# A hybrid attention layer on one core: an unused table of taps is dropped, x arrives in five first pieces, and every engine gets a new order of issue

## The chip, the cores and the metric

One core of a Trainium2 chip. The time is the device time of one execution in microseconds (us), the median of several runs. Before the change it is 332.9 us (3 runs, 332.89 to 332.98).

## The reference

One layer over 256 tokens of width 1024, in float32. The input is projected by one wide matrix, and the columns go to four mixers; their outputs are joined, projected, normed, and followed by a feed-forward stage of width 4096.

```python
h = x @ w_in
(q_n, kc, vc, ks, vs, kw, vw, g_n, q_m, k_m, v_m, conv_in, q_h, f_h, i_h, g_h) = split(h)
kc = nsa_compress(kc, cmp_pe[0], cmp_w1[0], cmp_b1[0], cmp_w2[0])    # and vc with [1]
o_nsa  = nsa_attention(q_n, kc, vc, ks, vs, kw, vw, sigmoid(g_n), rel_tab)
o_moba = moba_attention(q_m, k_m, v_m, rel_tab)
o_conv = conformer_conv(conv_in, dw_w, dw_b, cln_g, cln_b, pw_w)     # 31 taps, causal
o_hgrn = hgrn2_mixer(q_h, f_h, i_h, g_h, lb, hn_g)
mixed = concatenate([o_nsa, o_moba, o_conv, o_hgrn], -1) @ w_out
x = layer_norm(ALPHA * x + mixed, ln1_g, ln1_b)
ff = square(relu(x @ w_ff1)) @ w_ff2
return layer_norm(ALPHA * x + ff, ln2_g, ln2_b)
```

## The kernel before

**Stages.** The input projection is cut into chunks of columns (`ca`, `cg` for the convolution, `n1` and `ni` for the keys, values and gates, `qn`, `f`, `q`, `g`, `km`, `qm`, `vm`). Their products are mixed with the four mixers' own work up to about 130 us; then come `w_out`, the first norm, and 16 groups of the feed-forward stage, each a product with 256 columns of `w_ff1` and one with 256 rows of `w_ff2`.

**Precision.** Most weights and activations are split: ScalarE writes a rounded high part (`..._hi`, L245), VectorE the remainder (`..._lo`, L246), and TensorE takes three products per tile (L313 to L315 for transposed results, L335 to L337 for the chunk `ni`). The chunks `ca`, `cg`, `qn` and `km` are multiplied unsplit (L520, L310), as two passes each.

**Memory and queues.** A weight goes from HBM into one of five 1 MB buffers (the pool `raws`), requested from SyncE's queue (L228, and L424 for the two 1 MB pieces of each `nsa_cmp_w1`, `w1` for short). A buffer is free again when the last reader of its tenant is done: VectorE's remainder for a split weight, TensorE's last product for an unsplit one. x itself (`xf`) is requested from ScalarE's queue in four pieces (`FIRST`, L272), the first weight `w_ca` in the same four. GpSimd's queue loads the small constants, and among them `tapw`, a table of convolution taps of 1 MB which no instruction reads, since the convolution is done on VectorE (L573, 60 instructions of one tap each).

**Warm-up.** Seven products of a zeroed tile (L292) run on TensorE before the first piece of x is there.

**The first norm.** For each token tile t (two of them): two halves of x + mixed (L1014), their statistics (L1016, L1019), the inverse root of the variance (L1022 to L1026), a diagonal matrix `scale` of it (L1044), and two halves of (x - mean) * gain (L1042). TensorE then writes the norm's bias into PSUM by a small product (L1048, four in all, `pts[t][c]`), and adds x transposed and scaled on top (L1051, 16 products, each recorded as two rows). ScalarE (L1058) and VectorE (L1059) split the result for the feed-forward stage, which starts with L1089.

**Order.** Nothing is left to a scheduler: the table `ISSUE` lists for every engine the numbers of its instructions in the order in which they are issued, and `issue_in` ties each to the one before it. An engine works strictly in that order.

Of the kernel before, what the change touches and what calls it, by code (L numbers as in the profile page):

```python
# [17 lines left out]
P = 128  # L18
S = 256
# [27 lines left out]
def shape_constants():  # L47
# [13 lines left out]
    for i, b in enumerate(LEVELS):  # L61
# [48 lines left out]
    ),  # L110
    DVE=(
# [13 lines left out]
    ),  # L125
    Activation=(
# [9 lines left out]
    ),  # L136
# [1080 lines left out]
```

## Time and profile before

| | |
|---|---|
| median of 3 runs | 332.9 us |
| the profiled execution, its own time | 335.78 us |
| its span, first to last instruction | 334.0 us |
| TensorE (PE) busy | 319.8 us |
| VectorE (DVE) busy | 233.3 us |
| ScalarE (ACT) busy | 166.8 us |
| bytes moved by DMA | 62.75 MB |

The profiled execution took 2.9 us more than the median of the other runs. Starts of instructions are given in us from the span's start; an instruction's end on TensorE is modelled, and its rows overlap, so the start of the next row tells how fast they follow one another. "Idle before" in brackets is the time for which the engine had nothing under way, and behind the arrow stands what ended it.

### The profile page before, as it was taken

What the parts mean: (1) busy time and instruction counts of PE and PEld (TensorE: products, weight loads), DVE (VectorE), ACT (ScalarE), POOL (GpSimd) and SP (SyncE); (2) the same over time, 40 slices, a digit from 0 to 9 for tenths busy, and PEclk for the clock granted to TensorE, in tenths of its full rate; (3) what the DMA queues carried; (4) which work ended last, traced back from release to release, by engine and by line L of the source; (5) the groups of instructions that cost most, each with busy time, mean ns of one, the idle gap of its engine ahead of it and who ended that gap; (6) DMA issues with size and microseconds to landing.
All of it is one profiled execution on the core that took longest, in us unless ns stands there. A gap on an engine that the chain in (4) does not pass through costs nothing.

```text
span 334.0 us, 4992 instructions
## 1 busy us (share of the span) xinstructions
PE 319.8 (96%) x1929; PEld 273.1 (82%) x1929; DVE 233.3 (70%) x428; ACT 166.8 (50%) x307; POOL 10.5 (3%) x33
## 2 busy tenths in 40 slices
PE   8999969999999999989999999999999999999990
PEld 6897859898988778788888888888888888888880
DVE  0269969999989866886677477747564756568286
ACT  1464444784899982344365354535453545373100
POOL 3500000000000100000000000100000000000000
PEclk9999998999999999999999999999999999999996
DMA  7999799094300216556567555965565646520012
GB/s 234 387 398 416 235 395 388 15 371 135 121 0 2 54 74 251 153 226 186 214 232 251 176 203 155 318 202 207 153 226 160 219 144 233 156 98 0 2 49 77
DMA packets 18359, 62.75 MB, mean 188 GB/s; under 512 B 1784, under 2 KB 3664, under 8 KB 17696
## 3 DMA queue, kind: packets, MB, share of 16 engines
q1 hardware_dynamic: 15648, 56.61, 47.8%
q0 software_dynamic: 1056, 3.72, 3.2%
q10 hardware_dynamic: 1632, 2.11, 2.2%
q8 instruction: 15, 0.25, 0.3%
q14 instruction: 8, 0.07, 0.1%
HBM read 61.37 MB, written 1.06 MB: 187 GB/s over the span
## 4 chain that ended last, share of the span: by engine, by line
PE 86%; DVE 8%; DMA 2%; ACT 1%; issue 1%; DVEq 0%; ACTq 0%
PE mm L1102 15%; PE mm L1100 8%; PE hg L1121 5%; PE hg L1122 4%; PE tt L1122 4%; PE tt L1120 4%; PE hg L1120 4%; PE tt L1121 4%; DMA w_q_raw<-in_w_in_dram 2%; PE mm_km L310 2%; PE mm L1099 2%; PE mm_cg L310 2%; DVE yc L573 2%; PE acc L292 1%; PE tt L371 1%; PE tt L397 1%
## 5 line engine op out<-in xcount | busy, mean ns | idle before, releaser
L1102 PE MATMUL mm<-x1s,w_hi 128*128 128x512 f32 x210 | 74.4, 394 | 0.0
L246 DVE TENSOR_TENSOR r_lo<-r_raw,r_hi 128x1024 fp32r<-128x1024 f32 x40 | 47.4, 1221 | 24.8 <-ACT r_hi L245 24.8
L1100 PE MATMUL mm<-x1s,w_lo 128*128 128x256 f32 x240 | 61.0, 279 | 0.0
L245 ACT ACTIVATE r_hi<-r_raw 128x1024 fp32r<-128x1024 f32 x40 | 40.6, 1050 | 33.5 <-PE tt L1122 32.4
L1100 PEld LDWEIGHTS mm<-x1s,w_lo 128*128 128x128 f32 x240 | 44.9, 188 | 2.7
L1102 PEld LDWEIGHTS mm<-x1s,w_hi 128*128 128x128 f32 x210 | 39.2, 188 | 7.4
L246 DVE TENSOR_TENSOR w_lo<-w_raw,w_hi 128x1024 fp32r<-128x1024 f32 x32 | 37.8, 1218 | 5.0 <-ACT w_hi L245 5.0
L245 ACT ACTIVATE w_hi<-w_raw 128x1024 fp32r<-128x1024 f32 x32 | 32.2, 1051 | 4.6 <-DMA w_raw<-in_w_ff_dram 4.5
L1106 ACT ACTIVATE fx<-mm 128x256 f32<-128x256 f32 x30 | 11.4, 383 | 44.4 <-PE mm L1102 44.4
L1107 DVE TENSOR_TENSOR fs<-mm,fx 128x256 f32<-128x256 f32 x30 | 12.6, 424 | 28.5 <-ACT fx L1106 28.5
L573 DVE SCALAR_TENSOR_TENSOR yc<-hc,cols,yc 128x256 f32<-128x256 f32 x60 | 27.5, 479 | 0.5
L1121 PE MATMUL hg<-r_lo,fh 128*128 128x512 f32 (+1 forms) x70 | 26.4, 378 | 0.0
L1120 PE MATMUL hg<-r_hi,fh 128*128 128x512 f32 (+1 forms) x70 | 26.4, 377 | 0.0
L1121 PE MATMUL tt<-r_lo,fh 128*128 128x512 f32 x64 | 24.1, 396 | 0.0
L1122 PE MATMUL hg<-r_hi,fl 128*128 128x512 f32 (+1 forms) x70 | 22.4, 376 | 0.0
L1122 PE MATMUL tt<-r_hi,fl 128*128 128x512 f32 x64 | 20.8, 397 | 0.0
L1120 PE MATMUL tt<-r_hi,fh 128*128 128x512 f32 x64 | 20.8, 396 | 0.0
L1121 PEld LDWEIGHTS hg<-r_lo,fh 128*128 128x128 f32 x70 | 13.2, 189 | 2.7
L1122 PEld LDWEIGHTS hg<-r_hi,fl 128*128 128x128 f32 x70 | 13.2, 189 | 2.6
L1120 PEld LDWEIGHTS hg<-r_hi,fh 128*128 128x128 f32 x70 | 13.2, 188 | 2.1
L1121 PEld LDWEIGHTS tt<-r_lo,fh 128*128 128x128 f32 x64 | 12.1, 188 | 2.9
L1122 PEld LDWEIGHTS tt<-r_hi,fl 128*128 128x128 f32 x64 | 12.1, 189 | 2.8
(331 smaller groups left out, 650.7 us busy)
## 6 DMA issues: line engine op xcount, KB each, us to landing
w_raw<-in_w_ff_dram SPq DMA_DIRECT2D x32, 512.0 KB, 4.4
r_raw<-in_w_ff_dram SPq DMA_DIRECT2D x16, 1024.0 KB, 4.9
w<-in_nsa_cmp_w_dram SPq DMA_DIRECT2D x4, 1024.0 KB, 7.6
r_raw<-in_w_out_dram SPq DMA_DIRECT2D x4, 1024.0 KB, 6.1
w_ni_raw<-in_w_in_dram SPq DMA_DIRECT2D x2, 792.0 KB, 11.4
xf<-in_xt_dram ACTq DMA_DIRECT2D x4, 256.0 KB, 6.9
w_ca_raw<-in_w_in_dram SPq DMA_DIRECT2D x4, 256.0 KB, 7.1
w_cg_raw<-in_w_in_dram SPq DMA_DIRECT2D x2, 512.0 KB, 5.8
```

The lines of the kernel that those rows point to most:

```text
L245: A.activation(self.h[:, i:j], self.raw[:, i:j], AF.Copy)
L246: self.last = V.tensor_tensor(self.l[:, i:j], self.raw[:, i:j], self.h[:, i:j].bitcast(F32), op=ALU.subtract)
L310: T.matmul(dst[:, i], w.raw[:, k, P * i:P * i + P], xf[:, k], start=(k == 0), stop=(k == KT - 1))
L573: V.scalar_tensor_tensor(yc[:, i], h, w, yc[:, i], op0=ALU.mult, op1=ALU.add)
L1099: T.matmul(flat(pf[i]), h, flat(x1s[:, k]), start=True, stop=False)
L1100: T.matmul(pf[i][:, 0], l, x1h[:, k], start=False, stop=False)
L1102: T.matmul(flat(pf[i]), h, flat(x1s[:, k]), start=False, stop=(k == KT - 1))
L1106: A.activation(lo[:, i], pf[i][:, 1], AF.Copy)
L1107: V.tensor_tensor(sq[:, i], pf[i][:, 0], lo[:, i], op=ALU.add)
L1120: T.matmul(bank_, h, w.h[:, i, sl], start=(g == 0 and i == 0), stop=False)
L1121: T.matmul(bank_, h, w.l[:, i, sl], start=False, stop=False)
L1122: last = T.matmul(bank_, l, w.h[:, i, sl], start=False, stop=(g == NG - 1 and i == 1 and sl.stop != 768))
```

## The change

1. The table `taps`, its load and the branches that would read it are gone.
2. The first of the two 1 MB pieces of `w1` for c = 0 goes into the space that the table had (tag `mixl`), not into a buffer of `raws`, and it is requested much earlier, right behind `w_qn`.
3. x and `w_ca` come in five first pieces: two of one k-tile, three of two k-tiles.
4. There are five warm-up products where there were seven.
5. The last bias product of the first norm, (t, c) = (1, 1), is issued six times into the same PSUM bank. The first five start and end a group of their own, so that the sixth overwrites them.
6. `ISSUE` has a new table for all five engines.

```diff
-    FIRST, X_LATE = ((0, 2), (2, 4), (4, 6), (6, 8)), 2
+    FIRST, X_LATE = ((0, 1), (1, 2), (2, 4), (4, 6), (6, 8)), 2
...
-    for _ in range(7):
+    for _ in range(5):
         T.matmul(pidle, idle[:, :P], idle, start=True, stop=True)
...
-            raw = raws.tile([P, 2048], F32, name="w1", tag="raw").rearrange("p (a b) -> p a b", a=8)
+
+            pool, tag = (raws, "raw") if c or i else (wk, "mixl")
+            raw = pool.tile([P, 2048], F32, name="w1", tag=tag).rearrange("p (a b) -> p a b", a=8)
             nc.sync.dma_start(raw, I["nsa_cmp_w1"][:, c, i])
...
-    tapw = wk.tile([P, 8, 8, 32], F32, name="tapw", tag="mixl")
-    late(tapw, I["taps"])
...
         for c in range(2):
-            T.matmul(pts[t][c], bsum, bhot[:, 4 * c:4 * c + 4, None].to_broadcast([40, 4, P]), start=True, stop=False)
+            to = pts[t][c], bsum, bhot[:, 4 * c:4 * c + 4, None].to_broadcast([40, 4, P])
+
+            for _ in range(5 if (t, c) == (1, 1) else 0):
+                T.matmul(*to, start=True, stop=True)
+            T.matmul(*to, start=True, stop=False)
...
     SP=(
-        "0-10 30 28-29 11-27 31-89 "
+        "0-11 17 31 29-30 12-16 18-28 32-90 "
```

**SyncE's queue, the loads up to `w_km`.** Before (names `w_150` and `w_152` are the two pieces of `w1` for c = 0, `DMAHW` a wait for an earlier transfer, `PE` and `DVE` a wait for a buffer that these engines still read):

```order
L228 DMA w_qn_raw<-in_w_in_dram 128x1024 [waits DMAHW6_49]
L930 DMA pw<-in_conv_pw_w_dram 128x2x256 [waits DMAHW7_49]
L690 DMA w_687<-in_nsa_cmp_w_dram 128x128 [waits DMAHW0_49]
L692 DMA w2k<-in_nsa_cmp_w_dram 128x256 [waits DMAHW1_49]
L228 DMA w_f_raw<-in_w_in_dram 128x1024 [waits DMAHW2_49,PE_49]
L228 DMA w_f_raw<-in_w_in_dram 128x1024 [waits DMAHW3_49]
L228 DMA w_ni_raw<-in_w_in_dram 128x1584 [waits DMAHW4_49,PE_49]
L228 DMA w_qm_raw<-in_w_in_dram 128x1024 [waits DMAHW5_49,DVE_49]
L228 DMA w_qm_raw<-in_w_in_dram 128x1024 [waits DMAHW6_49]
L424 DMA w_150<-in_nsa_cmp_w_dram 128x2048 [waits DMAHW7_49,DVE_49]
L424 DMA w_152<-in_nsa_cmp_w_dram 128x2048 [waits DMAHW0_49,PE_49]
L228 DMA w_q_raw<-in_w_in_dram 128x1024 [waits DMAHW4_49,DMAHW2_49,DVE_49]
```

and now:

```order
L424 DMA w_150<-in_nsa_cmp_w_dram 128x2048 [waits DMAHW1_49]
L905 DMA pw<-in_conv_pw_w_dram 128x2x256 [waits DMAHW2_49]
L665 DMA w_685<-in_nsa_cmp_w_dram 128x128 [waits DMAHW3_49]
L667 DMA w2k<-in_nsa_cmp_w_dram 128x256 [waits DMAHW4_49]
L226 DMA w_f_raw<-in_w_in_dram 128x1024 [waits DMAHW5_49,PE_49]
L226 DMA w_f_raw<-in_w_in_dram 128x1024 [waits DMAHW6_49]
L226 DMA w_ni_raw<-in_w_in_dram 128x1584 [waits DMAHW7_49,DVE_49]
L226 DMA w_qm_raw<-in_w_in_dram 128x1024 [waits DMAHW0_49,PE_49]
L226 DMA w_qm_raw<-in_w_in_dram 128x1024 [waits DMAHW1_49]
L424 DMA w_152<-in_nsa_cmp_w_dram 128x2048 [waits DMAHW2_49,DVE_49]
L226 DMA w_q_raw<-in_w_in_dram 128x1024 [waits DMAHW4_49,PE_49]
L226 DMA w_q_raw<-in_w_in_dram 128x1024 [waits DMAHW6_49]
```

`w_150` needs no buffer of the pool any more, so each later load finds another buffer: `w_q` had waited for VectorE, which makes the remainder of the second half of `w_ni`, and now waits for TensorE's last product with `w_qn`.

**VectorE at the first norm, from the last halves of x + mixed (`mm` for t = 0, `tt` for t = 1) to the last (x - mean) * gain.** Before (`nw` the inverse root, `scale_1471` the diagonal of t = 0, `scale_1498` that of t = 1):

```order
L1019 BN_AGGR mv<-st 128x2
L1042 SCALAR_TENSOR_TENSOR x_1341<-x_1341,mv,gb 128x512 x2
L1014 SCALAR_TENSOR_TENSOR x_1341<-x_1341,tt 128x512
L1022 TENSOR_SCALAR nw<-mv 128x1
L1025 SCALAR_TENSOR_TENSOR nw<-nw 128x1
L1016 BN_STATS st<-x_1341 128x6
L1026 TENSOR_SCALAR nw<-nw 128x1
L1044 TENSOR_SCALAR scale_1471<-cc,nw 128x128
L1014 SCALAR_TENSOR_TENSOR x_1341<-x_1341,tt 128x512
```

and now (`scale_1469` is that of t = 0, `scale_1496` that of t = 1):

```order
L989 SCALAR_TENSOR_TENSOR x_1339<-x_1339,tt 128x512
L991 BN_STATS st<-x_1339 128x6
L994 BN_AGGR mv<-st 128x2
L1017 SCALAR_TENSOR_TENSOR x_1339<-x_1339,mv,gb 128x512
L997 TENSOR_SCALAR nw<-mv 128x1
L1000 SCALAR_TENSOR_TENSOR nw<-nw 128x1
L1001 TENSOR_SCALAR nw<-nw 128x1
L1019 TENSOR_SCALAR scale_1496<-cc,nw 128x128
L1001 TENSOR_SCALAR nw<-nw 128x1
L1019 TENSOR_SCALAR scale_1469<-cc,nw 128x128
L1017 SCALAR_TENSOR_TENSOR x_1339<-x_1339,mv,gb 128x512 x3
```

All of tile 0's work was done ahead of the last half of tile 1. Now both of its (x - mean) * gain and its `scale` stand behind `scale` of tile 1: the three at the end are t = 0, t = 1, t = 0. On TensorE the 16 products went tile 0 (`acc`, `hg`), then tile 1 (`hg`, `acc`); now they go tile 1 (`hg`), tile 0 (`hg`), tile 1 (`acc`), tile 0 (`acc`), behind the nine bias products.

On ScalarE around 30 us, before: both halves of `w_f_hi`, the copy of `qn` out of PSUM, then the high part of the second half of `w_ni`. Now that high part stands ahead of the copy of `qn`.

## Rows read from the trace of the kernel before

**Rows 1.** The page: busy time, share of the span and instructions of each engine.

```profile
PE 319.8 (96%) x1929; PEld 273.1 (82%) x1929; DVE 233.3 (70%) x428; ACT 166.8 (50%) x307; POOL 10.5 (3%) x33
```

**Rows 2.** Waits of TensorE, 0 to 150 us: line, waited for, total, times, longest.

```profile
PE mm_q L313 <- ACT iv L345: 2.6, 1, 2.6
PE hg L1051 <- DVE scale L1044: 1.3, 1, 1.3
```

**Rows 3.** Chain of waits, 25 to 60 us: start, us, what.

```profile
37.27 1.81 DVE w_ni_lo L246
39.10 7.20 DMA w_q_raw<-in_w_in_dram
46.40 1.06 ACT w_q_hi L245
```

**Rows 4.** Waits of SyncE's queue, 0 to 60 us.

```profile
SPq L228 <- DVE w_ni_lo L246: 5.8, 1, 5.8
```

**Rows 5.** Stretches: busy time by engine, granted clock, DMA share, GB/s.

```profile
28.00:34.00 6.00, 5.31 (x27) 4.46 (x26) 5.86 (x14) 4.47 (x8) 0.00 (x0) 1.00 1.03 398
...
46.00:48.00 2.00, 0.00 (x0) 0.00 (x0) 0.51 (x1) 1.56 (x5) 0.00 (x0) 1.00 1.04 420
48.00:50.00 2.00, 1.61 (x7) 1.61 (x8) 1.97 (x11) 2.00 (x8) 0.00 (x0) 0.61 1.01 408
...
60.00:100.00 40.00, 40.00 (x365) 36.43 (x366) 37.68 (x109) 30.68 (x72) 0.00 (x0) 1.00 0.36 133
```

**Rows 6.** TensorE, 30 to 54 us: start, us, line, what, [idle before].

```profile
33.53 0.45 PE L335 MATMUL mm_ni<-w_ni_hi,xs 128*128 128x396 f32 x1 [0.69 <-ACT qn L345]
...
43.48 1.93 PE L686 MATMUL acc<-w,blk 128*32 128x256 f32 x32
...
48.39 0.57 PE L313 MATMUL mm_q<-xs,w_q_hi 128*128 128x256 f32 x1 [2.55 <-ACT iv L345]
...
51.92 0.28 PE L313 MATMUL mm_f<-xs,w_f_hi 128*128 128x256 f32 x1
52.04 0.28 PE L314 MATMUL mm_q<-xs,w_q_hi 128*128 128x256 f32 x1
```

**Rows 7.** ScalarE, 31 to 35 us.

```profile
32.90 0.58 ACT L345 ACTIVATE qn<-mm_qn 128x512 f32<-128x512 f32 x1
...
33.53 1.53 ACT L245 ACTIVATE w_ni_hi<-w_ni_raw 128x1584 fp32r<-128x1584 f32 x1
```

**Rows 8.** DMA issues, 0 to 60 us: count, KB each, median us to landing.

```profile
w_ni_raw<-in_w_in_dram SPq DMA_DIRECT2D x2, 792.0 KB, 11.4
...
tapw<-in_taps_dram POOLq DMA_DIRECT2D x1, 1024.0 KB, 11.2
```

**Rows 9.** SyncE's queue: request of the second half of w_ni.

```profile
20.55 0.33 SPq L228 DMA_DIRECT2D w_ni_raw<-in_w_in_dram  x1
```

**Rows 10.** TensorE, 139 to 147 us.

```profile
139.56 0.39 PE L992 MATMUL tt<-r_hi,mixl 128*128 128x512 f32 x1
...
140.41 0.59 PE L1048 MATMUL hg<-bhot,bsum 40*128 40x512 f32 x2
...
144.36 1.16 PE L1051 MATMUL hg<-scale,x 128*128 128x128 f32 x8 [1.26 <-DVE scale L1044]
...
146.21 0.39 PE L1089 MATMUL mm<-x1s,w_hi 128*128 128x256 f32 x1
```

**Rows 11.** VectorE, 140 to 145 us.

```profile
140.91 0.68 DVE L1014 SCALAR_TENSOR_TENSOR x<-x,tt 128x512 f32<-128x512 f32 x1
...
143.96 0.35 DVE L1044 TENSOR_SCALAR scale<-cc,nw 128x128 f32<-128x128 f32 x1
144.22 0.74 DVE L1042 SCALAR_TENSOR_TENSOR x<-x,mv,gb 128x512 f32<-128x512 f32 x1
```

**Rows 12.** TensorE, 0 to 9 us.

```profile
1.19 4.69 PE L292 MATMUL acc<-idle 128*128 128x256 f32 x14 [1.19 <-DVE idle L289]
5.72 0.67 PE L520 MATMUL mm<-xf,w_ca_raw 128*128 128x256 f32 x2
```

More of the change, by code (lines that the diff above doesn't have):

```diff
@@ L70 @@
     PE=(
[39 rows of a table removed]
[39 rows of a table added]
     ),
     DVE=(
[13 rows of a table removed]
[13 rows of a table added]
     ),
     Activation=(
[9 rows of a table removed]
[9 rows of a table added]
     ),
     Pool=(
-        "20-22 14 23-24 15 2 9-10 13 11-12 0-1 3-8 16-19 25-28 "
+        "19-21 13 22-23 14 2 8-9 12 10-11 0-1 3-7 15-18 24-27 "
     ),
     SP=(
-        "0-10 30 28-29 11-27 31-89 "
+        "0-11 17 31 29-30 12-16 18-28 32-90 "
     ),
@@ L180, in layer @@
     PLAIN = ("ca", "km", "cg", "qn")
-    CONV_T = ()
     LOADS = "ca cg n1 ni0 qn f ni1 qm w1a q km g w1b vm".split()
@@ L539, in part_conv @@
     def part_conv():
-        nonlocal pcv, yc
+        nonlocal yc
         at_(K["taps"])
         yc = t2_("c", "yc")
-        if CONV_T:
-            W, H, n = 28 + S, 31 + S, len(CONV_T)
-            hc_d = dr.tile([P, n, H], F32, name="hc_d")
-            G.dma_start(hc_d, hc[:, CONV_T[0]:CONV_T[0] + n])
-            hcs = wk.tile([P, n, 4, W], F32, name="hcs", tag="hgw")
-            for i in range(n):
-                for j in range(4):
-                    G.dma_start(hcs[32 * j:32 * j + 32, i],
-                                bass.AP(tensor=hc_d.tensor, offset=hc_d.offset + i * H + j,
-                                        ap=[[n * H, 32], [32 * n * H, 4], [1, W]]))
-            pcv = hbank([P, n, S])
-            for i in range(n):
-                for b in range(8):
-                    for q in range(4):
-                        T.matmul(pcv[32 * q:32 * q + 32, i], tapw[:, 4 * CONV_T[i] + q, b], hcs[:, i, q, 4 * b:4 * b + S],
-                                 start=(b == 0), stop=(b == 7))
-            for i, c in enumerate(CONV_T):
-                A.activation(yc[:, c], pcv[:, i], AF.Identity, bias=cols[:, R_DB + c:R_DB + c + 1])
         at_(K["tapv"])
@@ L565, in part_conv @@
             for i in range(2):
-                if i in CONV_T:
-                    continue
                 w = cols[:, R_DW + 2 * k + i:R_DW + 2 * k + i + 1]
@@ L1181, in lay_out @@
                            for r, i, j in CHUNKS.values()], axis=1)
-    dw = a["conv_dw_w"][0]
-    taps = np.zeros((4, 32, 8, 8, 32), np.float32)
-    for k in range(31):
-        for c in range(32):
-            taps[(k + 1) % 4, c, :, (k + 1) // 4, c] = dw[k, c::32]
     brow = np.zeros((40, P), np.float32)
@@ L1192, in lay_out @@
     ff1 = a["w_ff1"][0].reshape(8, P, 16, 256).transpose(1, 2, 0, 3)
-    out = dict(x=a["x"], xt=tiles(a["x"][0].T), w_in=w_in, cols=rows.T, taps=taps.reshape(P, 8, 8, 32), brow=brow,
+    out = dict(x=a["x"], xt=tiles(a["x"][0].T), w_in=w_in, cols=rows.T, brow=brow,
                nsa_cmp_w1=w1, nsa_cmp_w2=w2, rel_bias=a["rel_bias"].T, w_ff1=ff1)
```

122 rows, old and new, of tables (Activation, DVE, PE) are left out of this document.

## The prediction

> **What bounds the kernel now.** The busy times come first: TensorE is busy 319.8 of 334.0 us, VectorE 233.3 [rows 1]. So a change can pay only where TensorE stands still or runs slowly, and the reader should look for those places next. The waits of TensorE up to 150 us name two of size: 2.6 us before the first product with `w_q` and 1.3 us in the first norm [rows 2]. A third, 0.69 us, stands before `mm_ni` [rows 6]. The chain of waits says where the longest comes from [rows 3]: VectorE makes the remainder of the second half of `w_ni` at 37.27 us, only then is a buffer free, the request for `w_q` leaves at 39.10 us, the data take 7.20 us, and ScalarE makes the high part at 46.40 us. SyncE's queue shows the same place from the other side: it stood 5.8 us for that remainder [rows 4]. The stretches tell the second half of the cost: TensorE did nothing from 46 to 48 us, and in the next 2 us its granted clock was 0.61, between its two levels of 1.2 and 2.4 GHz [rows 5]. The products' own rows agree: they follow each other at 0.12 us from 51.92 us on, but from 48.39 to 51.92 us there are 16 rows, 0.22 us apart [rows 6].
>
> All durations are from the profiled execution, which took 335.78 us; the median of the other runs is 332.9 us, 2.9 us less. The sum is a difference within that one execution, and I take it off the median, as none of its terms is a place where the two can be seen to differ.
>
> **Removed: the stall for `w_q`.** The first piece of `w1` leaves the pool, every later load moves up by one buffer, and `w_q` now takes the one of `w_qn`, which is free when TensorE has done its last product with it. That is before the copy of `qn` at 32.90 us [rows 7], so the request leaves at about 33 us, 6 us earlier than at 39.10 us. With the same 7.20 us it lands at about 40 us (its second half a little later). TensorE gets to `mm_q` at 48.39 - 2.55 = 45.84 us [rows 6]. In the new order ScalarE copies the four results of `mm_ni` first and then makes the high part, 1.06 us [rows 3]. Before, the copies ran between the end of the high part at 47.46 us and 48.39 us, 0.9 us. The products of `mm_ni` end where those of `w1` begin, at 43.48 us [rows 6], so the high part is there at 45.5 us, still ahead of TensorE, by 0.4 us. What is late next is VectorE's remainder of `w_q`, needed 15 products on, or 15 x 0.12 = 1.8 us; it takes about as long as its high part. So the stall goes whole: **-2.5 us**. Bounds: 0, if another wait stands there, and -3.0 us, if the small attention products that now lie elsewhere in the order close their gaps too.
>
> With the stall goes the slow stretch: 16 rows in 51.92 - 48.39 = 3.53 us, at 0.12 us they need 1.9 us: **-1.6 us** [rows 6].
>
> The Trainium skill has the mechanism ("TensorE: Matmul & The Clock Gate", section "What's actually happening"): the array's clock is gated by how busy TensorE has been recently. The trace agrees: no product from 46 to 48 us, 0.61 in the 2 us after them [rows 5].
>
> **The loads themselves.** The table of taps moved 1 MB [rows 8] from GpSimd's queue, and the 1 MB of `w1` is now requested at much the same place of the queue of transfers. From 28 to 34 us the 16 DMA engines are full, share 1.03 at 398 GB/s [rows 5]. So up to then the bytes ahead of `w_f` and `w_ni` are as many as before, and I book nothing; 1 MB at 398 GB/s would be 2.6 us of landing time if the exchange were not even.
>
> The Trainium skill says ("Trainium Kernel Development and Optimization", section "Key Constraints") that transfers from SyncE's, ScalarE's and GpSimd's queues run on the same 16 engines and interleave. By that rule a table dropped from GpSimd's queue would speed SyncE's loads, and a piece of `w1` put ahead of them takes the same back. The trace shows the full engines; that they share is borne out by it only so far as all loads slow down together.
>
> **Added: ScalarE's split ahead of the copy of `qn`.** TensorE starts `mm_ni` when `qn` is copied, and waited 0.69 us there [rows 6]. Now the second high part of `w_ni`, 1.53 us, goes first [rows 7]. It needs its data: requested at 20.55 us, 11.4 us to landing [rows 8, 9], so 32.0 us. Before the change it found them at 33.53 us without a wait. A landing half a us to either side, 31.5 to 32.5 us, plus 1.53 and 0.58 us, gives a copy that is done at 33.6 to 34.6 us, and TensorE had started at 33.53 us [rows 6]. I take the early end, **+0.1 us**, because by the count of bytes the data land no later than before; bounds -0.2 and +1.0 us.
>
> **The start.** Two warm-up products are four rows of the 14, which take 4.5 us up to 5.72 us [rows 12]: 1.3 us by their mean. The first piece of x is half as large, so it may land that much sooner. But the third piece now ends where the second ended before, at the same number of bytes; TensorE would get there earlier and wait. Later it waits for `qn` in any case. Booked at **0**, bounds -1.3 and +0.4 us (one more request per queue ahead of the later pieces).
>
> **The middle, 46 to 134 us.** All of it is reordered. From 60 to 100 us TensorE is busy 40.00 of 40 us and VectorE 37.68 [rows 5]. The number of products is the same, so with the products back to back the stretch is moved as a whole and nothing comes of it: **0**. Cover: VectorE gains too, since its idle time before the remainder of `w_q` goes as well. If the cover is gone, VectorE sets the pace (a rival below). Bounds -0.5 and +1.5 us.
>
> **The first norm gets longer.** Before: the last product of `w_out` starts at 139.56 us, the feed-forward stage at 146.21 us, 6.65 us later [rows 10]. Tile 0's eight products lay in the time in which VectorE worked on tile 1. Now they wait for work that VectorE does behind tile 1's `scale`.
> First what is gained: VectorE's last half of x + mixed began at 140.91 us [rows 11], late, since tile 0's `scale` was in its way. Now it has 0.68 us for the half before, 0.7 for its statistics; that is done about 0.4 us after TensorE's end (139.95 us), so tile 1's `scale` moves from 143.96 to about 143.4 us, 0.5 us earlier.
> Then what is lost: counted from the end of that `scale`, tile 1's first four products take 0.95 us (16 rows from 144.36 to 146.21 us are 1.85 us, [rows 10]). VectorE meanwhile needs 0.25 + 0.35 us for the other `scale` and 0.7 us for a half of x, so tile 0's four start at 1.3 and end at 2.3 us; the next eight follow without a wait, to 4.1 us. Before, it was 1.9 us from there to the feed-forward stage. Lost 2.2, gained 0.5: **+1.6 us**, rounded down a little. Bounds: 0 and +2.5 us.
> The five extra bias products take 5 x 0.25 = 1.2 us (two are recorded with 0.59 us, [rows 10]) and lie in the time in which TensorE waits for `scale`: from 140 to 143.8 us it has nine of them, 2.2 us, and then stands 1.6 us. Cost 0; 1.2 us if that gap were gone.
>
> **Sum:** -2.5 - 1.6 + 0.1 + 1.6 = -2.4 us. Forecast 332.9 - 2.4 = **330.5 us**. The feed-forward stage and the end are the same.
>
> **The rivals.**
> 1. *The clock falls at the norm.* A stand of 1.26 us left it up, one of 2.55 us did not [rows 6, 10]; 1.6 us lies between. If it falls, about as many us as at `mm_q` run slowly: +1.6 us, 332.1 us. Against it: the extra bias products keep TensorE at work until shortly before.
> 2. *VectorE sets the pace in the middle.* It is busy 37.68 of 40 us [rows 5], and TensorE comes 4 us earlier than it did. If VectorE keeps only the part of the gain that was its own idle time, 2.4 us are given back: 332.9 us, no change. Against it: no wait of TensorE for VectorE over 0.2 us up to 134 us is among its waits.
> 3. *Slower: the second half of `w_ni` lands late.* ScalarE then waits for it with the copy of `qn` behind it, and TensorE has nothing else to issue. Every us of landing is one of TensorE. It decides from about 1.9 us on, when the stand is as long as the one of 2.55 us that brought the clock down: +1.9 and +1.6 us, together 334.0 us. For it: the engines are full there; against it: the count of bytes.
> 4. *The norm costs nothing*, since tile 0's products find other cover: 328.9 us.
> 5. *The new order does not remove the stall*, as `w_q` lands late behind 1 MB more: then only the norm's loss is left, 334.5 us. Against it: 5 us of room.
>
> **The numbers.** Forecast 0.52; rival 1 0.14; rival 2 0.12; rival 3 0.07; rival 4 0.10; rival 5 0.05. The forecast's own range from its bounds is 329.3 to 331.6 us. Over all cases 328.5 to 333.2 us: it leaves out rivals 3 and 5 and some of 4. About 0.2% (0.67 us) is what can be told from no change. Faster by more than that: the forecast nearly whole (0.50), rival 1 (0.12), rival 4 (0.10), a third of rival 2 (0.04): 0.76. Within it: 0.12. Slower: 0.12.
>
> **What would show it.** No wait of TensorE between the end of `w1`'s products and `mm_q`, and a clock of 1.00 from 44 to 52 us; the request of `w_q` at about 33 us; a wait for `qn` of 0.7 to 1.4 us; 8.2 us from the last `w_out` product to the feed-forward stage with one stand of about 1.6 us in it; TensorE busy throughout from 50 to 134 us. Wrong it is if TensorE waits for VectorE in the middle, if the clock is under 1.00 behind the norm, or if the start is a whole us shorter.

## The result, and the profile after

The changed kernel takes 335.64 us (median of 4, 335.30 to 336.75), the one before 332.89 us beside it (4 executions, 332.21 to 332.98): a ratio of 1.0093, 95% interval 1.0064 to 1.0121. It is slower by 0.9%; 2.4 us less had been forecast. The profiled execution took 336.75 us, the longest of the four, with a span of 335.0 us. Further down, one of ten executions of `b_norm` and one of 102 of before count as slow: they stand in the medians and in no ratio.

TensorE's waits up to 160 us, in the changed kernel (line, what it waited for, total, times, longest):

```profile
PE mm_n L313 <- DVE w_n_lo L244: 1.5, 1, 1.5
PE hg L1030 <- DVE nw L1001: 1.3, 1, 1.3
...
PE mm_ni L333 <- ACT qn L343: 0.7, 1, 0.7
PE acc L878 <- DVE hgw L863: 0.5, 1, 0.5
```

The stand for `w_q` [rows 2] is not there, as forecast. A new one of 1.5 us stands before `mm_n`, in the first 20 us, where no wait was forecast. The wait for `qn` is as long as it was [rows 6]. A small one, for `hgw`, is new in the middle.

The same places as TensorE's rows (start, us, line, what, [idle before]):

```profile
18.75 0.28 PE L312 MATMUL mm_n<-xs,w_n_hi 128*128 128x256 f32 x1
20.49 0.39 PE L313 MATMUL mm_n<-xs,w_n_lo 128*128 128x256 f32 x1 [1.47 <-DVE w_n_lo L244]
...
46.93 0.39 PE L311 MATMUL mm_q<-xs,w_q_hi 128*128 128x256 f32 x1
...
137.59 0.39 PE L967 MATMUL tt<-r_hi,mixl 128*128 128x512 f32 x1
...
138.66 1.25 PE L1026 MATMUL acc<-bhot,bsum 40*128 40x512 f32 x5
...
141.48 3.18 PE L1030 MATMUL hg<-scale,x 128*128 128x128 f32 x16 [1.35 <-DVE nw L1001]
144.45 2.55 PE L1030 MATMUL acc<-scale,x 128*128 128x128 f32 x16
146.76 0.36 PE L1068 MATMUL mm<-x1s,w_hi 128*128 128x256 f32 x1
```

`mm_q` starts at 46.93 us, 1.5 us earlier than in the trace of before, and at full pace: the granted clock is 1.00 from 44 to 52 us. `w_q` was requested at 34.50 us, where about 33 us had been forecast:

```profile
34.50 0.81 SPq L226 DMA_DIRECT2D w_q_raw<-in_w_in_dram  x2
```

But the norm, from the last product of `w_out` to the feed-forward stage, takes 146.76 - 137.59 = 9.17 us where it took 6.65 us [rows 10]. The first 16 rows behind the stand take 2.97 us, where 16 rows took 1.85 us [rows 10]. The stretches say why (busy time of TensorE, its weight loads, VectorE, ScalarE, GpSimd, then granted clock, DMA share, GB/s):

```profile
137.00:141.00 4.00, 3.13 (x14) 2.08 (x12) 3.75 (x10) 1.52 (x4) 0.00 (x0) 1.00 0.91 318
141.00:145.00 4.00, 3.52 (x19) 3.48 (x20) 3.38 (x8) 1.84 (x3) 0.00 (x0) 0.66 0.94 379
145.00:149.00 4.00, 4.00 (x34) 4.00 (x34) 3.22 (x5) 3.15 (x5) 0.00 (x0) 0.91 0.00 0
```

TensorE stood for 1.35 us, and then its clock was granted at 0.66 of 2.4 GHz over 4 us: part of them at 1.2 GHz.

### The profile page after: what moved, and what is told of

Its sections match the earlier page's. It is cut to its first block, busy times and chain, and to the rows that moved or that the text cites. A ratio compares the mean times of both kernels' runs of the same rounds, so it can differ in the third digit from the quotient of the medians.

```text
span 335.0 us, 4993 instructions
## 1 busy us (share of the span) xinstructions
PE 320.6 (96%) x1930; PEld 273.6 (82%) x1930; DVE 234.5 (70%) x428; ACT 167.7 (50%) x307; POOL 10.0 (3%) x32
## 3 DMA queue, kind: packets, MB, share of 16 engines
HBM read 60.32 MB, written 1.06 MB: 183 GB/s over the span
## 4 chain that ended last, share of the span: by engine, by line
PE 81%; DVE 9%; DMA 5%; ACT 2%; issue 1%; SPq 0%; DVEq 0%
PE mm L1081 15%; PE mm L1079 8%; PE hg L1100 5%; PE hg L1101 4%; PE tt L1101 4%; PE hg L1099 4%; PE tt L1099 4%; PE tt L1100 4%; DMA w_qn_raw<-in_w_in_dram 3%; PE mm_km L308 2%; PE mm L1078 2%; PE mm_qn L308 2%; DMA w_ca_raw<-in_w_in_dram 2%; PE acc L661 1%; PE tt L369 1%; PE mm L965 1%
## 5 line engine op out<-in xcount | busy, mean ns | idle before, releaser
L1099 PEld LDWEIGHTS tt<-r_hi,fh 128*128 128x128 f32 x64 | 12.1, 189 | 2.9
```

The lines of the kernel that those rows point to most:

```text
L1099: T.matmul(bank_, h, w.h[:, i, sl], start=(g == 0 and i == 0), stop=False)
```

## The experiments

Some of the kernels are made of whole stages of the two orders: since both tables name the same instructions but for the few that the change adds or drops, the order of one can be kept up to a point and that of the other taken from there on. The medians are each beside executions of the kernel before on the same chip.

### The kernel before, once more: `b_again`

No edit.

> The kernel before, unchanged, to see a second trace of it. Theory 1 (the first trace is typical, what it lost at w_q is lost in every execution): the profiled execution again near 335.8 us, with a stand of about 2.5 us before mm_q and a clock under 1.00 at 48 to 52 us, and a profiled time above the timed runs by about 3 us for a reason common to all profiles. Theory 2 (the first profiled execution was an unlucky one): a profiled time near the median of 332.9 us, and no or a shorter stand before mm_q, or a full clock behind it.

332.27 us (10 executions, 331.49 to 332.78) beside 332.45 us (19). The profiled execution took 332.78 us, span 331.0 us: 3.0 us less than the first trace. In its waits nothing stands before `mm_q`. SyncE's queue waited 5.8 us for VectorE's remainder, as in [rows 4], but the transfer was quicker. SyncE's queue, ScalarE, the transfers of `w_q`, and TensorE in this second trace:

```profile
40.13 0.80 SPq L228 DMA_DIRECT2D w_q_raw<-in_w_in_dram  x2
```

```profile
DMA to landing us min/median/max: 4.3/4.9/5.4
```

```profile
44.62 1.06 ACT L245 ACTIVATE w_q_hi<-w_q_raw 128x1024 fp32r<-128x1024 f32 x1 [2.64 <-PE mm_ni L337]
```

```profile
46.38 0.49 PE L371 MATMUL tt<-ksw,qn 64*128 64x128 f32 x4
46.80 0.39 PE L313 MATMUL mm_q<-xs,w_q_hi 128*128 128x256 f32 x1
```

The request leaves at 40.13 us, later than in [rows 3], yet the first half is there 4.3 us on, at 44.4 us, where the first trace had 7.20 us. ScalarE does not wait for it at all: it waits for TensorE's last product of `mm_ni`. So the 2.5 us stand and the 1.6 us of slow products belong to one execution in which `w_q` came late; theory 2 holds. Why that transfer was slow is not shown. Of the 102 executions of before that were timed beside the experiments, 98 are within 331.5 to 333.9 us; of the other four, three have a mean clock of 0.987 or 0.988, near the 0.986 of the first trace. Such executions exist, but they are rare.

The start differs too. The 14 rows of warm-up take 6.06 us here and not 4.69 us [rows 12], 0.43 us apart, where the rows of the first products with x, as long, follow at 0.22 us. The granted clock reads 1.00 in both traces from 0 to 10 us, so the lower clock is inferred from the spacing and not read:

```profile
1.19 6.06 PE L292 MATMUL acc<-idle 128*128 128x256 f32 x14 [1.19 <-DVE idle L289]
7.09 0.59 PE L520 MATMUL mm<-xf,w_ca_raw 128*128 128x256 f32 x2
```

This second trace is the one to compare with. Starts of products on TensorE in us, the first of a stage where nothing else is said, each from that row of the trace:

| | before, first trace | before, second | after | m_rest2 |
|---|---|---|---|---|
| first product with x | 5.72 | 7.09 | 5.74 | 5.40 |
| `mm_n` | 18.37 | 19.42 | 18.44 | 18.81 |
| `mm_ni` | 33.53 | 34.55 | 35.16 | 33.78 |
| `mm_q` | 48.39 | 46.80 | 46.93 | 45.56 |
| last product of `mm_q` | 63.08 | 59.97 | 59.66 | 58.30 |
| last product of `w_out` | 139.56 | 136.54 | 137.59 | 135.26 |
| feed-forward stage | 146.21 | 143.19 | 146.76 | 141.91 |

Against the second trace the changed kernel is 1.35 us ahead at the start, level at `mm_q` (+0.13), behind by 1.05 us at the end of `w_out` and by 3.57 us at the feed-forward stage. At the end of the span it is 4.0 us behind, so another 0.4 us are lost in or behind the feed-forward stage. They lie behind VectorE's last rows, here of the second trace of before and of the changed kernel:

```profile
326.53 1.54 DVE L1169 SCALAR_TENSOR_TENSOR x<-x,nw,gb 128x512 f32<-128x512 f32 x3
330.14 1.54 DVE L1148 SCALAR_TENSOR_TENSOR x<-x,nw,gb 128x512 f32<-128x512 f32 x3
```

From their start to the end of the span it is 331.0 - 326.53 = 4.5 us and 335.0 - 330.14 = 4.9 us. All ten traces of kernels that have the changed kernel's loads and its order up to `mm_q` show 4.8 to 4.9 us there, all seven others 4.4 to 4.5 us, `b_q` below among them. What in these loads or this order does it was not tested.

### The early load alone, in the kernel before: `b_q`

```diff
-            raw = raws.tile([P, 2048], F32, name="w1", tag="raw").rearrange("p (a b) -> p a b", a=8)
+            pool, tag = (raws, "raw") if c or i else (wk, "mixl")
+            raw = pool.tile([P, 2048], F32, name="w1", tag=tag).rearrange("p (a b) -> p a b", a=8)
...
-    tapw = wk.tile([P, 8, 8, 32], F32, name="tapw", tag="mixl")
-    late(tapw, I["taps"])
```

> The kernel before, with the table of taps gone and the first piece of w1 in its space, all orders of issue unchanged. Theory 1 (the stand for w_q with the slow stretch behind it is in every execution of before): the request for w_q leaves at about 33 us, the stand goes, and the time falls by 3 to 4 us to 329 to 330 us. Theory 2 (typical executions of before lose less at w_q than the traced one): it falls by 0 to 2 us, 331 to 333 us.

332.07 us beside 332.45 us, ratio 0.9989 (0.9976 to 1.0001). `mm_q` starts at 46.93 us. The part of the change that carried the forecast is worth nothing that can be told from no change: in a typical execution `w_q` was not late. Theory 2 again.

### `selr` moved back, in the changed kernel: `a_selr`

```diff
     DVE=(
-        "19 0-1 24 98 2 5-6 3-4 7 22-23
+        "19 0-1 24 2 5-6 3-4 7 22-23
...
-        8 49 10 42 44
+        8 49 10 98 42 44
```

> The changed kernel with one instruction moved on VectorE: selr, which needs the constants cc from GpSimd's queue and stands ahead of three splits in the new order, goes back behind the second remainder of w_ni, as before the change. Theory: the 1.5 us for which TensorE waited for w_n_lo at 19 us go, and 1.0 to 1.5 us of them reach the end: 334.1 to 334.6 us. Rival: TensorE waits as long for qn or for mm_q's high part instead, and the time stays at 335.6 us.

335.43 us, ratio 1.0090 (1.0073 to 1.0107) to before. In the trace the wait for `w_n_lo` is gone and `w_out` ends at 136.53 us, 1.06 us earlier; in the time hardly any of it is seen, as the norm behind it differs from execution to execution: the mean clock is 0.986 or 0.987 in all four of `a_selr`, and 0.991 or 0.992 in two of the changed kernel's four. The next pair measures it where the norm does not.

### The changed kernel up to `mm_q`, the order of before from there on: `m_rest`, `m_rest2`, and `m_selr`

Everything of the change up to the last product of `mm_q`, `selr` moved back; behind it the old order on all engines, and one bias product where there were six. `m_rest2` is the same kernel, and `m_selr` is it with `selr` in its new place.

> The changed kernel up to the last product of mm_q (five first pieces, five warm-up products, the new loads and the new order, with selr moved back), and from there on the order of before on every engine, the norm's too, without the five extra products. Theory (the new order of the middle costs 1.3 us, the norm 2.5 us, and the start gains 1 us if selr is not in the way): 331.2 to 331.8 us, under the 332.4 us of before. Rival (the middle's order costs nothing; what is gained early is lost wherever VectorE or ScalarE set the pace): 332.2 to 333.0 us.

> The kernel of m_rest once more, as the base of the next two and to see whether it beats before: 331.4 to 332.0 us, against 332.4 us of before.

> m_rest with one instruction moved back to where the changed kernel has it: selr, which waits for the constants, ahead of three splits on VectorE. Theory (TensorE stands 1.2 to 1.5 us for w_n_lo, and behind it only TensorE sets the pace): 1.0 to 1.3 us over m_rest, 332.7 to 333.0 us. Rival (VectorE makes it good later): no difference, 331.7 us.

`m_rest` 331.74 us beside 332.51 us, ratio 0.9974 (0.9949 to 0.9999); `m_rest2` 331.88 us beside 332.45 us, 0.9987 (0.9975 to 0.9999); `m_selr` 332.63 us, 1.0005 (0.9993 to 1.0018). So `selr`'s place costs 332.63 - 331.88 = 0.75 us here, and the first 58 us of the change without it are a small gain: `m_rest` lies under both kernels, though only just clear of the interval. VectorE in the changed kernel shows the mechanism:

```profile
18.51 0.19 DVE L675 TENSOR_TENSOR selr<-cc 128x32 f32<-128x32 f32 x1 [4.55 <-DMA cc<-in_const_dram]
18.61 0.68 DVE L457 TENSOR_TENSOR xs<-xf,xs 128x512 fp32r<-128x512 f32 x1
19.22 2.35 DVE L244 TENSOR_TENSOR w_n_lo<-w_n_raw,w_n_hi 128x1024 fp32r<-128x1024 f32 x2
```

`selr` takes 0.19 us, and TensorE reads it first at 64 us, but it reads the constants `cc`, the last large load of GpSimd's queue. VectorE stands 4.55 us for them with the remainders of x and of `w_n` behind it. In `m_rest2` the same two are done piece by piece from 14.05 us on:

```profile
14.05 0.69 DVE L461 TENSOR_TENSOR xs<-xf,xs 128x512 fp32r<-128x512 f32 x1 [0.36 <-ACT xs L460]
```

The size is not the same everywhere. `a_norm` and `a_both` below also differ by `selr` alone, and their medians by 334.49 - 332.87 = 1.62 us, on two chips and with four executions of `a_norm`; and in a second trace of the changed kernel (`a_again`) TensorE waits 0.4 us for `w_n_lo` and not 1.5 us.

### The middle alone: `a_both`

The changed kernel with `selr` back and the old norm: its order differs from that of `m_rest2` only between the last product of `mm_q` and the norm.

> The changed kernel with selr moved back and the first norm in the order of before, without the extra products: it differs from m_rest only in the order between the last product of mm_q and the norm. Theory (the new order of the middle costs 1.0 to 1.5 us, in stands of TensorE for VectorE and ScalarE between 90 and 110 us): 332.7 to 333.3 us. Rival (the middle costs nothing, all of the rest was the norm): 331.7 us.

332.87 us, ratio 1.0016 (1.0004 to 1.0027): 332.87 - 331.88 = 0.99 us for the order of the middle. The stretches of `a_both` in which TensorE loses time:

```profile
80.00:90.00 10.00, 9.78 (x78) 8.97 (x77) 9.57 (x35) 8.95 (x26) 0.00 (x0) 1.00 0.61 208
90.00:100.00 10.00, 9.78 (x113) 7.88 (x112) 9.01 (x20) 9.28 (x22) 0.00 (x0) 1.00 0.02 6
100.00:110.00 10.00, 9.47 (x104) 7.78 (x100) 9.71 (x31) 9.35 (x26) 0.00 (x0) 1.00 0.00 1
```

and of `m_rest2`:

```profile
80.00:90.00 10.00, 10.00 (x98) 9.39 (x96) 9.55 (x34) 8.55 (x28) 0.00 (x0) 1.00 0.19 76
90.00:100.00 10.00, 10.00 (x115) 8.20 (x114) 8.15 (x26) 9.88 (x24) 0.00 (x0) 1.00 0.01 2
100.00:110.00 10.00, 9.96 (x93) 8.12 (x93) 9.81 (x31) 9.52 (x31) 0.38 (x1) 1.00 0.00 1
```

TensorE's idle time there is 0.22 + 0.22 + 0.53 = 0.97 us; in `m_rest2` it is 0.04 us. From the last product of `mm_q` to that of `w_out` `a_both` takes 0.98 us longer. The waits of `a_both` name the places:

```profile
PE acc L1034 <- DVE scale L1023: 0.5, 1, 0.5
PE acc L882 <- DVE hgw L867: 0.5, 1, 0.5
...
PE acc L741 <- DVE pc L738: 0.2, 1, 0.2
PE mm L918 <- ACT ysq L915: 0.2, 1, 0.2
```

The first of them lies behind the middle, in the norm: VectorE comes later out of the new middle, and tile 0's `scale` with it, so that the old norm takes 7.15 us here and 6.65 us in `m_rest2`. In the traces the middle therefore costs 0.98 + 0.50 us. `a_both` ends only 1.0 us behind because at the last product of `mm_q`, in the same order up to there, it happened to be 0.55 us ahead (57.75 against 58.30 us). So 0.99 us may be too little for the middle with the old norm; with the new one the 0.50 us do not show (`a_noextra2` below).

### The norm alone: `a_norm`, `b_norm`, `b_norm10`, `a_noextra`

`a_norm` gives the changed kernel the old norm without extra products, `b_norm` gives the kernel before the new one with five, `b_norm10` with ten, and `a_noextra` takes the five out of the changed kernel. In the kernel before, of `b_norm10`:

```diff
-            T.matmul(pts[t][c], bsum, bhot[:, 4 * c:4 * c + 4, None].to_broadcast([40, 4, P]), start=True, stop=False)
+            to = pts[t][c], bsum, bhot[:, 4 * c:4 * c + 4, None].to_broadcast([40, 4, P])
+            for _ in range(10 if (t, c) == (1, 1) else 0):
+                T.matmul(*to, start=True, stop=True)
+            T.matmul(*to, start=True, stop=False)
```

> The changed kernel with the first norm in the order of before on TensorE, VectorE and ScalarE, and without the five extra bias products. Theory: from the last product of w_out to the feed-forward stage 6.65 us again and not 9.17 us, with a full clock: 333.1 us. Rival 1 (the clock falls here whatever the order, since the stand is now before other work): 334 to 334.6 us. Rival 2 (the extra products are needed): 335.6 us or more.

> The kernel before with the first norm alone in the new order, and with the five extra bias products. Theory (the norm is the largest loss, 2.5 us, as the traces have 6.65 us from the last product of w_out to the feed-forward stage before and 9.17 us after): 334.6 to 335.2 us against 332.4 us. Rival (the norm's loss in the changed kernel comes from what arrives late out of the middle, not from its order): 332.4 to 333.2 us.

> The kernel of b_norm with ten extra bias products, so that TensorE's stand ahead of the 16 products is filled but for 0.2 us. It separates the two parts of the norm's loss. Theory (the order costs about 0.9 us and the fall of the clock 1.5 us or more, and the clock falls because of the stand): a full clock in the norm and 333.3 us in every execution. Rival 1 (the clock falls whatever is done, as these small products count for little): 334.9 us, as with five. Rival 2 (the ten delay the products): 334 us with a full clock.

> The changed kernel without the five extra bias products, its order unchanged. Theory (the clock falls at this norm with or without them, since VectorE's chain sets the stand): 335.3 to 336.0 us, no difference. Rival 1 (they keep part of the clock): 1 us or more slower, 336.5 us. Rival 2 (they delay the 16 products): 334.8 us or less.

`a_norm` 334.49 us, 1.0063 (1.0047 to 1.0079): 1.1 us under the changed kernel, less than the 2.5 us that I expected, though its clock is 1.00 throughout the norm: that takes 7.14 us, as in `a_both`, and `selr` stands in its new place. `b_norm` 334.90 us beside 332.51 us, 1.0058 (1.0022 to 1.0094), with nine executions from 332.76 to 336.35 us and one of 339.74 us: those with a mean clock of 0.992 or 0.993 took 332.8 to 333.9 us, those from 0.984 to 0.988 took 334.8 to 336.4 us, the longest has 0.983. `b_norm10` 333.28 us beside 332.45 us, 1.0037 (1.0019 to 1.0054), ten of its twelve executions with 0.992 or 0.993. The norm of `b_norm10`, TensorE, VectorE with the `scale` of tile 1, and the stretches:

```profile
135.46 0.39 PE L997 MATMUL tt<-r_hi,mixl 128*128 128x512 f32 x1
...
136.53 2.34 PE L1055 MATMUL acc<-bhot,bsum 40*128 40x512 f32 x10
138.72 0.38 PE L1056 MATMUL acc<-bhot,bsum 40*128 40x512 f32 x1
139.35 2.27 PE L1059 MATMUL hg<-scale,x 128*128 128x128 f32 x16 [0.26 <-DVE nw L1031]
141.45 1.95 PE L1059 MATMUL acc<-scale,x 128*128 128x128 f32 x16
143.16 0.36 PE L1097 MATMUL mm<-x1s,w_hi 128*128 128x256 f32 x1
```

```profile
138.95 0.34 DVE L1049 TENSOR_SCALAR scale<-cc,nw 128x128 f32<-128x128 f32 x1
```

```profile
136.00:140.00 4.00, 3.75 (x19) 2.97 (x19) 3.67 (x11) 0.50 (x2) 0.00 (x0) 1.00 0.90 325
140.00:144.00 4.00, 4.00 (x36) 3.86 (x35) 3.72 (x6) 3.46 (x6) 0.00 (x0) 1.00 0.63 254
```

and the same stretches of `b_norm`:

```profile
136.00:140.00 4.00, 2.78 (x12) 1.79 (x10) 3.67 (x11) 1.10 (x3) 0.00 (x0) 0.93 0.95 323
140.00:144.00 4.00, 3.87 (x18) 3.87 (x19) 3.16 (x7) 1.59 (x3) 0.00 (x0) 0.50 0.82 333
```

With ten extra products TensorE stands 0.26 us and keeps its clock; with five it stands 1.35 us, and the clock is at 0.50 for the next 4 us. So the norm's loss has two parts: the order itself, 333.28 - 332.45 = 0.83 us (1.05 us in the trace, 7.70 us for the norm where 6.65 us were [rows 10]), and the clock. That is another 334.90 - 333.28 = 1.6 us between the medians, taken on two chips. In a single execution in which the clock falls it is more or less: the norm takes 9.17 us in the changed kernel's trace and 10.41 us in `b_norm`'s, 1.5 and 2.7 us over 7.70 us.

The extra products of the change do not prevent that. Without them TensorE stands 2.45 us in `a_noextra`:

```profile
140.64 3.25 PE L1032 MATMUL hg<-scale,x 128*128 128x128 f32 x16 [2.45 <-DVE nw L1003]
```

and its time, 336.49 us (ratio 1.0111), was not taken beside the changed kernel. So both ran again, side by side:

> The changed kernel once more, as the base of the next one on the same chip: 335.3 to 336.0 us.

> The changed kernel without the five extra bias products, beside the changed kernel on the same chip. Theory (five are too few to keep the clock, so they neither cost nor give): within 0.4 us of it. Rival (they shorten the slow stretch in some executions): 0.6 to 1.2 us slower than it.

336.75 us with them (336.08 to 338.39), 336.07 us without (335.37 to 337.30), ratios 1.0123 (1.0082 to 1.0165) and 1.0100 (1.0060 to 1.0141). They give nothing that can be seen; whether they cost anything stays open, as the intervals overlap.

But the stand alone does not bring the clock down. In the trace of `a_noextra2`, the same kernel as `a_noextra`, TensorE stands as long, and the clock stays up:

```profile
137.66 0.39 PE L969 MATMUL tt<-r_hi,mixl 128*128 128x512 f32 x1
...
141.56 2.27 PE L1032 MATMUL hg<-scale,x 128*128 128x128 f32 x16 [2.44 <-DVE nw L1003]
143.66 1.95 PE L1032 MATMUL acc<-scale,x 128*128 128x128 f32 x16
145.37 0.36 PE L1070 MATMUL mm<-x1s,w_hi 128*128 128x256 f32 x1
```

```profile
141.00:145.00 4.00, 3.44 (x28) 3.31 (x29) 3.64 (x9) 2.25 (x4) 0.00 (x0) 1.00 0.95 386
```

The norm takes 7.71 us there, as in `b_norm10`: a second measure of what the order costs alone. How often the clock falls can be counted, since the mean clock of an execution tells it: the six profiled executions with a stretch below 1.00 have 0.984 to 0.988, the other eleven 0.990 or more, and none of the executions counted here lies between.

| norm | extra products | executions with 0.988 or less |
|---|---|---|
| old (`a_norm`, `a_both`, `m_rest`, `m_rest2`, `m_selr`) | 0 | 0 of 50 |
| new (`a_noextra`, `a_noextra2`) | 0 | 12 of 16 |
| new (changed kernel, `a_selr`, `a_again`, `b_norm`) | 5 | 19 of 24 |
| new (`b_norm10`) | 10 | 2 of 12 |

So it is the new norm that lets the clock fall, in most executions and not in all, and five products do not change that. Ten do, as far as one chip shows it: `b_norm10` ran on that one only.

### Five warm-up products, in the kernel before: `b_idle5`, `b_idle5_2`

```diff
-    for _ in range(7):
+    for _ in range(5):
```

> The kernel before with five warm-up products instead of seven, nothing else. Theory (TensorE gets to its first product with x 0.9 to 1.3 us earlier, as the two products take four rows of 0.22 or 0.43 us, and the first pieces are there): 331.2 to 331.8 us. Rival (the second piece of x lands at 7.4 us whatever is done, and TensorE waits for it): 332.2 to 332.6 us.

> The kernel before with five warm-up products, once more. Theory (TensorE waits for VectorE's blk in mm_ni for most of what it gains at the start, and four of the rows are worth 0.9 us at the most): 0.2 to 0.4 us under before. Rivals: nothing; or 0.9 us and more, as the first stage starts 1.4 us earlier in the trace.

332.20 us beside 332.51 us, ratio 1.0000 (0.9965 to 1.0035), and 332.26 us beside 332.54 us, 0.9989 (0.9965 to 1.0013): 0.3 us less in both medians, and no change by the interval. In the trace the first product with x starts at 5.67 us, 1.4 us earlier than in `b_again`; how much of it is the two products and how much the wider spacing of the warm-up rows in `b_again` is not separated.

## Why the prediction was wrong

**The stand for `w_q`, -2.5 - 1.6 us, is the step that failed.** Its mechanism was read rightly: the buffer does come free earlier, and no stand is left. But there is none in a typical execution of before either (`b_again`), and the early load alone is worth nothing (`b_q`). The prediction noted that the profiled execution was 2.9 us over the median and went on that "none of its terms is a place where the two can be seen to differ". Just there they differed: one execution had `w_q` 7.20 us on the way, the other 4.3 us. From the first product of `mm_ni` to the last of `mm_q` the first trace takes 63.08 - 33.53 = 29.55 us and the second 59.97 - 34.55 = 25.42 us: 4.1 us less, just the two terms. So they were sized rightly for that one execution, but booked on a median that does not have them. Without them the forecast would have been 332.9 + 0.1 + 1.6 = 334.6 us: slower, and 1 us short of what was measured.

**The start, 0.** Its order was not walked on VectorE. There one instruction waits for a constant ahead of the remainders of x and `w_n`: 0.75 us in the time (`m_selr` against `m_rest2`), 1.6 us in a weaker pair. What the rest of the first 58 us brings is 331.88 - 332.45 = -0.57 us by `m_rest2`, with the 0.4 us of its longer end in it; the fewer warm-up products alone were not told from no change.

**The middle, 0 with bounds to +1.5 us.** It is +0.99 us by the medians (`a_both` against `m_rest2`). TensorE is so densely busy there that three waits of 0.2 to 0.5 us count in full, two of them for VectorE and one for ScalarE. It is a weak form of the rival in which VectorE sets the pace.

**The norm, +1.6 us.** The order costs 0.83 us and not 1.6 us (`b_norm10`), so this term was sized too high. In the trace without the fall VectorE begins tile 1's `scale` 138.95 - 135.46 = 3.5 us behind the start of the last product of `w_out`, and 143.96 - 139.56 = 4.4 us before the change [rows 10, 11]: 0.9 us are gained, where 0.5 us had been taken. But the clock fell as well (`b_norm`, and the rows after), which had been the first rival, with 1.6 us for it. Together they make 2.4 us. I had taken a stand of 1.6 us behind the five products as one that leaves the clock alone; the stand was 1.35 us, and in most executions the clock fell.

**`qn`, +0.1 us, and the loads, 0.** As forecast: the wait is 0.7 us as before, and the changed kernel's trace has no wait of TensorE for a load up to `mm_q`.

**The end, "the same".** It is 0.4 us longer in all ten traces of kernels with the changed kernel's loads; what causes it stays open.

A slip in the rivals: the sum of rival 5 leaves out the 0.1 us for `qn`: it gives 334.6 us and not 334.5 us.

**The sum.** Trace against trace it closes. The changed kernel's profiled execution took 336.75 - 332.78 = 3.97 us more than `b_again`'s: 0.13 us at `mm_q`, 0.92 us more at the end of `w_out`, 2.52 us in the norm (1.05 us for the order, 1.47 us with the slow clock) and 0.4 us at the end. It was the longest of four; the two with a mean clock of 0.991 and 0.992, in which by the count above the clock did not fall, took 335.32 and 335.30 us, 1.4 us less. So the median, 335.64 us, lies between executions of two kinds. That is one reason why the 335.64 - 332.89 = 2.75 us measured are less than the medians of the pieces add up to: -0.57 + 0.75 + 0.99 + 0.83 + 1.6 = +3.6 us.

## What to carry to other kernels

Before a gain is read from a trace, compare the profiled execution with the median: if it is longer by as much as the largest wait, look at a second trace of the same kernel before that wait is booked: here 4.1 us of gain rested on it, more than the whole forecast. When an engine's order is rewritten, look for the first instruction on it that needs a late load, however small, and at all that is queued behind it. And a stand ahead of small products is paid twice where the clock falls: five products that left 1.35 us of it open did not make that rarer, and ten that left 0.26 us kept the clock up in ten of twelve executions.

## What was not expected of the hardware

TensorE's clock did not follow the length of a stand alone. With the old norm it stayed up in every trace, behind a stand of 1.26 us with tile 0's eight products (16 rows) done ahead of it, here in `b_again`:

```profile
138.02 1.16 PE L1051 MATMUL acc<-scale,x 128*128 128x128 f32 x8
139.02 1.06 PE L1051 MATMUL hg<-scale,x 128*128 128x128 f32 x8
141.34 1.16 PE L1051 MATMUL hg<-scale,x 128*128 128x128 f32 x8 [1.26 <-DVE scale L1044]
```

It fell behind one of 1.35 us after nine bias products, in most executions but not in all (`b_norm`). And behind a stand of 2.4 us it fell in one trace of a kernel (`a_noextra`, 9.12 us for the norm) and stayed at 1.00 in another trace of the same kernel (`a_noextra2`, 7.71 us). What decides between the two is not shown. At the start, the same seven warm-up products took 4.69 us in one execution and 6.06 us in another, at two spacings of their rows.
